# A batched trace of a matrix product: TensorE's transposes in 2-byte words with register-held addresses, and loops on three engines

## The chip, the cores and the metric

The kernel runs on one core of a Trainium2 chip. The core has five engines with instruction streams of their own, which meet through semaphores: TensorE (PE in the profile; its weight loads are shown as PEld), VectorE (DVE), ScalarE (ACT), GpSimd (POOL) and SyncE (SP). Sixteen DMA engines move data between HBM and the on-chip memory SBUF. PE writes into PSUM, which VectorE and ScalarE read. The metric is device time in microseconds; before the change it is 708.59 us, the median of 3 runs (708.46 to 708.78).

## What is computed

```python
B, N = 8, 2176
a, b: float32 [B, N, N]

prod = np.matmul(a, b)
traces = np.diagonal(prod, axis1=1, axis2=2).sum(axis=-1)   # float32 [B]
```

The trace of a product needs no product: it is the sum over i and k of a[i, k] * b[k, i]. So each element of A has to meet the element of B at the transposed place. All of A and B, 303 MB, is read once.

## The kernel before

N is 17 blocks of P = 128 rows. They come in three groups: the first 5 blocks are the "middle" (MID = 5), the other 12 are two "side" groups of 6 (SIDE = 6, MOST = 12). Within a group of m blocks, partition p holds m consecutive rows of the matrix, so that a transfer reads long runs of HBM. The transfers cast from float32 to bf16 on the way. SBUF tiles: `middle` (5 rows of 2176 per partition; it holds A's middle first and then B's middle of the same batch), `a_side` and `b_side` (12 rows each), and `at` (17 x 2176 per partition), which holds A transposed.

For each of the 8 batches:

1. POOL issues four transfers in this order: A's middle, A's side, B's middle, B's side. Each has to wait until its tile has been read: A's middle for the previous batch's product over `middle` (L160, 161), A's side for the previous batch's last transposes (L164, 165), B's middle for this batch's transposes of `middle` (L178, 179), B's side for the previous batch's second product (L183, 187). All are on one queue, in that order.
2. SP passes landings on to PE: `mid_in` when A's middle is there, `all_in` when the side is there (L139 to 145).
3. PE transposes A in a loop over the batches (L298 to 308). Its body is 26 "fills" of a PSUM tile; there are three such tiles (BUFS), released by `free0` to `free2`. For the column groups with an even number of blocks, two neighbouring bf16 numbers are taken as one 4-byte word, so that one 128 x 128 transpose moves 128 x 256 numbers; the 5 columns of the odd group go in 2-byte words. All addresses are constants. A batch has 55 transposes for the middle (8 fills) and 132 for the side (18 fills).
4. ScalarE and VectorE copy each fill into `at` (L218), ScalarE three of four, VectorE the fourth. Neither starts before both products of the previous batch are done (L217). Then each drains and adds to `at_done` (L219). Their streams are written out for all 8 batches.
5. VectorE multiplies `at` with B and sums, in one instruction per part: first with `middle` (10,880 elements per partition), then with `b_side` (26,112), L255 to 259, each sum into a column of `sums`. Each adds one to `product`.

The last batch is different, to have little left when the last byte lands. B's side comes in slices (LATE_SLICES) and the last row in three pieces (LAST_PIECES). VectorE takes some rows, and PE takes the others by accumulating matmuls of 128 x 128 blocks into `trace_ps`, whose diagonal VectorE sums (L286). The list `work` (L315 to 347) holds PE's 122 matmuls and 21 fillers (KEEP_BUSY) between them, matmuls of 512 columns into a PSUM tile that nobody reads. At the end a matmul with `ones` adds up over the partitions and SP writes the result.

## Time and profile before

| | us | where |
|---|---|---|
| median of 3 runs | 708.59 | times |
| the profiled execution | 708.71 | times |
| its span, first to last instruction | 706.6 | page |
| VectorE busy | 380.2 (54%) | page, 1 |
| PE matmul busy | 207.3 (29%) | page, 1 |
| ScalarE busy | 202.3 (29%) | page, 1 |
| HBM read | 303.04 MB, 429 GB/s | page, 3 |
| product over `b_side`, 26,112 elements | 27.36 | groups by form |
| product over `middle`, 10,880 elements | 11.49 | groups by form |
| copy of 1536 / 1280 elements, ScalarE | 1.46 / 1.23 | groups by form |
| copy of 1536 elements, VectorE | 1.76 | groups by form |

Shares are of the span. The granted clock of TensorE is 0.651 of full speed on average. A line of a timeline has the start, the time, the engine, the source line, the operation with what it writes and reads, and in brackets how long the engine sat idle before and what ended that.

### The profile page before, as it was taken

What the parts mean: (1) busy time and instruction counts of PE and PEld (TensorE: products, weight loads), DVE (VectorE), ACT (ScalarE), POOL (GpSimd) and SP (SyncE); (2) the same over time, 40 slices, a digit from 0 to 9 for tenths busy, and PEclk for the clock granted to TensorE, in tenths of its full rate; (3) what the DMA queues carried; (4) which work ended last, traced back from release to release, by engine and by line L of the source; (5) the groups of instructions that cost most, each with busy time, mean ns of one, the idle gap of its engine ahead of it and who ended that gap; (6) DMA issues with size and microseconds to landing.
All of it is one profiled execution on the core that took longest, in us unless ns stands there. A gap on an engine that the chain in (4) does not pass through costs nothing. (4 is left out here: it accounts for less than half of the span.)

```text
span 706.6 us, 3944 instructions
## 1 busy us (share of the span) xinstructions
PE 207.3 (29%) x1641; PEld 188.0 (27%) x1643; DVE 380.2 (54%) x96; ACT 202.3 (29%) x158; POOL 25.0 (4%) x47
## 2 busy tenths in 40 slices
PE   0325003450134501334013430125301353012647
PEld 0224002440123401234013430125301352012535
DVE  0105488154871539715396163961639617395268
ACT  1427002370034700246004450044500454004540
POOL 1000000000000000000000000000000000002000
PEclk9759555695557955678555785556855677555678
DMA  9999999999999999999999999999999999999997
GB/s 228 222 213 207 229 211 213 217 223 214 223 218 213 209 227 211 213 218 222 210 231 213 210 218 219 214 214 226 214 215 225 213 208 228 208 217 214 226 206 151
DMA packets 7686, 152.13 MB, mean 215 GB/s; under 512 B 642, under 2 KB 898, under 8 KB 1410
## 3 DMA queue, kind: packets, MB, share of 16 engines
q0 software_dynamic: 7536, 150.96, 99.7%
q1 hardware_dynamic: 146, 1.11, 0.5%
q8 instruction: 2, 0.03, 0.0%
q14 instruction: 2, 0.02, 0.0%
HBM read 303.04 MB, written 0.00 MB: 429 GB/s over the span
## 5 line engine op out<-in xcount | busy, mean ns | idle before, releaser
L218 ACT COPY at<-fill 128x1536 bf16<-128x1536 bf16 (+3 forms) x156 | 199.9, 1371 | 472.2 <-DVE sums L231 357.0
L231 DVE CUSTOM_DVE_ANT_0 at<-at,b_side 128x26112 bf16<-128x26112 bf16 (+4 forms) x11 | 202.9, 18460 | 84.1 <-DMA b_side<-in_b_dram 84.1
L218 DVE COPY at<-fill 128x1536 bf16<-128x1536 bf16 (+2 forms) x52 | 84.0, 1615 | 220.6 <-PE fill L307 220.2
L307 PE MATMUL fill<-identity,middle 128*128 128x128 f32 (+1 forms) x440 | 69.0, 341 | 371.3 <-PEq L305 371.2
L307 PEld LDWEIGHTS fill<-identity,middle 128*128 128x128 f32 (+1 forms) x440 | 63.5, 180 | 376.5 <-issue 376.2
L307 PE MATMUL fill<-identity,a_side 128*128 128x128 f32 (+1 forms) x1056 | 123.6, 276 | 113.4 <-PEq L305 112.8
L307 PEld LDWEIGHTS fill<-identity,a_side 128*128 128x128 f32 (+1 forms) x1056 | 113.4, 166 | 123.7 <-issue 123.3
L231 DVE CUSTOM_DVE_ANT_0 at<-at,middle 128x10880 bf16<-128x10880 bf16 x8 | 91.9, 11491 | 11.0 <-ACTq L219 11.0
L179 POOL DMA_DIRECT2D middle<-in_b_dram x8 | 4.5, 561 | 335.1 <-PE fill L307 335.1
L161 POOL DMA_DIRECT2D middle<-in_a_dram x7 | 3.9, 563 | 292.4 <-DVE sums L231 292.4
L344 PE MATMUL trace_ps<-b_side,at 128*128 128x128 bf16 x122 | 10.3, 253 | 9.4 <-DMA b_side<-in_b_dram 9.3
L344 PEld LDWEIGHTS trace_ps<-b_side,at 128*128 128x128 bf16 x122 | 9.3, 116 | 11.3 <-DMA b_side<-in_b_dram 10.9
L165 POOL DMA_DIRECT2D a_side<-in_a_dram x8 | 5.7, 711 | 0.0
L187 POOL DMA_DIRECT2D b_side<-in_b_dram x7 | 5.0, 711 | 0.0
L344 PE MATMUL fill<-at 128*128 128x512 bf16 x19 | 4.8, 379 | 0.1
L246 DVE CAST middle<-b_side 128x1088 bf16<-128x1088 f32 x1 | 0.7, 726 | 5.0 <-DMA b_side<-in_a_dram 5.0
L344 PEld LDWEIGHTS fill<-at 128*128 128x128 bf16 x21 | 1.9, 98 | 1.5
L222 ACT CAST middle<-b_side 128x1088 bf16<-128x1088 f32 x1 | 1.1, 1099 | 3.9 <-DMA b_side<-in_a_dram 3.9
L198 POOL DMA_DIRECT2D b_side<-in_b_dram x4 | 2.1, 563 | 0.0
L203 POOL DMA_DIRECT2D b_side<-in_b_dram x3 | 1.6, 593 | 0.0
L222 ACT ACT_TABLE_LOAD x1 | 1.3, 1283 | 0.9 <-SPq L135 0.9
L231 DVE DVE_READ_ACCUMULATOR2_ANT sums<- 128x1 f32 x14 | 1.2, 83 | 0.0
(17 smaller groups left out, 4.2 us busy)
## 6 DMA issues: line engine op xcount, KB each, us to landing
a_side<-in_a_dram POOLq DMA_DIRECT2D x8, 6528.0 KB, 54.6
b_side<-in_b_dram POOLq DMA_DIRECT2D x7, 6528.0 KB, 52.2
middle<-in_b_dram POOLq DMA_DIRECT2D x8, 2720.0 KB, 22.1
middle<-in_a_dram POOLq DMA_DIRECT2D x7, 2720.0 KB, 24.5
b_side<-in_b_dram POOLq DMA_DIRECT2D x1, 3264.0 KB, 37.2
middle<-in_a_dram POOLq DMA_DIRECT2D x1, 2176.0 KB, 14.8
b_side<-in_b_dram POOLq DMA_DIRECT2D x3, 544.0 KB, 46.5
b_side<-in_a_dram SPq DMA_DIRECT2D x1, 1088.0 KB, 5.1
```

The lines of the kernel that those rows point to most:

```text
L161: nc.gpsimd.dma_start(out=middle.rearrange("p (g r) k -> p g (r k)", g=1), in_=group(a[bi], 0, 1, MID),).then_inc(sem["a_mid"], 16)
L165: nc.gpsimd.dma_start(out=a_side.rearrange("p (g r) k -> p g (r k)", g=2), in_=group(a[bi], MID * P, 2, SIDE),).then_inc(sem["a_all"], 16)
L179: nc.gpsimd.dma_start(out=middle.rearrange("p (g r) k -> p g (r k)", g=1), in_=group(b[bi], 0, 1, MID),).then_inc(sem["b_mid"], 16)
L187: nc.gpsimd.dma_start(out=b_side.rearrange("p (g r) k -> p g (r k)", g=2), in_=group(b[bi], MID * P, 2, SIDE),).then_inc(sem["b_all"], 16)
L198: nc.gpsimd.dma_start(out=b_side[:, SIDE + r:SIDE + r + m, :].rearrange("p r k -> p (r k)"), in_=rows[:, r:r + m, :].rearrange("p r k -> p ...
L203: nc.gpsimd.dma_start(out=b_side[:, MOST - 1, lo:hi], in_=rows[:, SIDE - 1, lo:hi],).then_inc(sem[f"piece{len(LATE_SLICES) + k}"], 16)
L218: copy(out=dst, in_=src).then_inc(sem[f"free{i % BUFS}"], 1)
L222: nc.scalar.copy(out=middle[:, MID - 1, :half], in_=plain[:, :half]).then_inc(sem["cast"], 1)
L231: return nc.vector.tensor_tensor_reduce(out=x if out is None else out, in0=x, in1=y, scale=1.0, scalar=0.0, op0=MUL, op1=ADD, accum_out=acc,)
L246: nc.vector.tensor_copy(out=middle[:, MID - 1, half:], in_=plain[:, half:]).then_inc(sem["cast"], 1)
L307: done = nc.tensor.transpose(into, block, identity)
L344: done = nc.tensor.matmul(trace_ps if real else fill_tiles[0][:, 0:4, :], x, y, start=(n == 0 or not real), stop=(n == len(work) - 1 or no ...
```

## The change

TensorE's transposes. The tiles `middle` and `a_side` become parts of one tile `rows_a` of 18 rows: the five rows of the middle, a row of zeros, and the twelve of the side. PE loops over the batches and, inside, over 9 passes of two rows (PAIR = 2; three passes for the middle, six for the side). A pass fills three PSUM tiles, `unit0` to `unit2`, one for each column group, with 2-byte transposes alone: 34 in a pass, 306 in a batch. The address that a transpose reads is the loop's register plus a constant. Each pass takes one count of `rows_in`, of which SP gives 3 when A's middle has landed and 6 when the side has.

The copies. ScalarE copies all three units of the middle's passes and `unit0` and `unit1` of the side's; VectorE copies `unit2` of the side's. ScalarE's eight batches are one loop, and VectorE's first seven another; before, each batch's instructions were written out. POOL's waits are on `mid_read` and `side_read`, which ScalarE and VectorE give, in place of PE's count `filled`.

The products. The product over `b_side` is cut into the first 640 columns (LOW) and the rest. `low_free` follows the first part and lets ScalarE start on the middle's passes of the next batch, `act_free` follows the second and lets it start on the side's. Three sums go into `part` and are copied to `sums`. VectorE learns of B's landings through SP (`b_mid_in`, `b_all_in`).

The last batch. PE's matmuls for B's late rows become loops over the columns, a pass taking one 128 x 128 block of each row of the slice, with both operands' addresses from the loop's register; the fillers have loops of their own. The last row's 12 matmuls stay written out.

```diff
-    BUFS = 3
-    DVE_EVERY = 4
+    PAIR = 2
+    STEPS = (MID + 1 + MOST) // PAIR
+    MID_STEPS = (MID + 1) // PAIR
+    LOW = MID * P
...
-    a_side = sb.tile([P, MOST, N], bf16, tag="a_side")
+    rows_a = sb.tile([P, PAIR * STEPS, N], bf16, tag="rows_a")
+    middle, a_side = rows_a[:, 0:MID, :], rows_a[:, MID + 1:, :]
...
+    def take(engine, name, n=1):
+
+        engine.wait_ge(sem[name], n).then_inc(sem[name], -n)
...
+    def unit_copy(copy, j, step):
+
+        v, cols = columns[j]
+        row = PAIR * step
+        group_at, m, r = (0, MID, row) if step < MID_STEPS else divmod_side(row - MID - 1)
+        n = min(PAIR, m - r)
+        dst = at[:, v:v + cols, group_at:group_at + P * m].rearrange("q v (p r) -> q v p r", r=m)
+        src = units[j][:, 0:cols * PAIR, :].rearrange("q (c r) p -> q c p r", r=PAIR)
+        copy(out=dst[:, :, :, r:r + n], in_=src[:, :, :, 0:n]).then_inc(sem[f"free{j}"], 1)
...
-        for bi in range(BATCH):
-            evacuate(nc.scalar, nc.scalar.copy, bi, False)
+        with nc.Fori(0, BATCH, engines=(ACT,)):
+            take(nc.scalar, "low_free")
+            for step in range(STEPS):
+                if step == MID_STEPS:
+                    take(nc.scalar, "act_free")
+                for j in range(len(units) if step < MID_STEPS else len(units) - 1):
+                    take(nc.scalar, f"filled{j}")
+                    if step == MID_STEPS - 1 and j == len(units) - 1:
+                        nc.scalar.sem_inc(sem["mid_read"], 1)
+                        nc.scalar.sem_inc(sem["mid_copied"], 1)
+                    unit_copy(nc.scalar.copy, j, step)
+            nc.scalar.drain().then_inc(sem["at_done"], 1)
...
+        with nc.Fori(0, n_sums - PARTS + 1, PARTS, engines=(DVE,)) as column0:
+            copies_on_dve()
+            take(nc.vector, "b_mid_in")
+            rows_product(0, middle, part[:, 0:1]).then_inc(sem["product"], 1)
+            take(nc.vector, "b_all_in")
+            multiply_reduce(
+                at[:, MID:NT, 0:LOW], b_side[:, :, 0:LOW], part[:, 1:2],
+            ).then_inc(sem["product"], 1)
+            nc.vector.drain().then_inc(sem["low_free"], 1)
+            multiply_reduce(
+                at[:, MID:NT, LOW:], b_side[:, :, LOW:], part[:, 2:3],
+            ).then_inc(sem["product"], 1)
+            nc.vector.drain().then_inc(sem["act_free"], 1)
+            nc.vector.tensor_copy(
+                out=sums[:, bass.ds(column0, PARTS)], in_=part
+            ).then_inc(sem["kept"], 1)
...
+            with nc.Fori(0, PAIR * (STEPS - 1) * N + 1, PAIR * N, engines=(PE,)) as row0:
+                take(nc.tensor, "rows_in")
+                for j, (v, cols_j) in enumerate(columns):
+                    take(nc.tensor, f"free{j}")
+                    start, step = B_GROUPS[j]
+                    for c in range(cols_j):
+                        for r in range(PAIR):
+                            done = nc.tensor.transpose(
+                                units[j][:, c * PAIR + r, :],
+                                flat[:, bass.ds(row0 + (r * N + start + c), P, step=step)],
+                                identity16,
+                            )
+                    done.then_inc(sem[f"filled{j}"], 1)
...
+            def block(flat_, row):
+                at0 = c + row * N
+                return flat_[:, at0:at0 + P] if isinstance(c, int) else flat_[:, bass.ds(at0, P)]
...
+        def multiply_on_pe(landed, rows, lo, hi, busy=0):
+
+            nc.tensor.wait_ge(sem[landed[0]], landed[1])
+            with nc.Fori(lo, hi - P + 1, P, engines=(PE,)) as c:
+                for v in rows:
+                    product(v, c)
+            if busy:
+                with nc.Fori(0, busy, engines=(PE,)):
+                    x = at[:, rows[-1], :]
+                    nc.tensor.matmul(fill, x[:, 0:P], x[:, 0:4 * P], start=True, stop=True)
```

More of the change, by code (lines that the diff above doesn't have):

```diff
@@ L47 @@
     at = sb.tile([P, NT, N], bf16, tag="at")
-    a_side = sb.tile([P, MOST, N], bf16, tag="a_side")
+    rows_a = sb.tile([P, PAIR * STEPS, N], bf16, tag="rows_a")
+    middle, a_side = rows_a[:, 0:MID, :], rows_a[:, MID + 1:, :]
     b_side = sb.tile([P, MOST, N], bf16, tag="b_side")
-    middle = sb.tile([P, MID, N], bf16, tag="middle")
     identity32 = sb.tile([P, P], f32, tag="identity32")
@@ L54 @@
     ones = sb.tile([P, 1], f32, tag="ones")
-    sums = sb.tile([P, 2 * (BATCH - 1)], f32, tag="sums")
+    PARTS = 3
+    sums = sb.tile([P, PARTS * (BATCH - 1)], f32, tag="sums")
+    part = sb.tile([P, PARTS], f32, tag="part")
     late_acc = sb.tile([P, NT], f32, tag="late")
     result = sb.tile([P, BATCH], f32, tag="result")
-    fill_tiles = [ps.tile([P, 8, P], f32, tag=f"fill{j}", name=f"fill{j}") for j in range(BUFS)]
+    units = [ps.tile([P, PAIR * 8, P], bf16, tag=f"unit{j}", name=f"unit{j}") for j in range(len(B_GROUPS))]
     trace_ps = ps.tile([P, P], f32, tag="trace")
-    total = ps.tile([1, 2 * (BATCH - 1) + NT], f32, tag="total")
+    total = ps.tile([1, PARTS * (BATCH - 1) + NT], f32, tag="total")
     sem = {}
@@ L72 @@
         semaphore(f"piece{k}")
-    for name in ("cleared", "constant", "cast", "mid_in", "all_in", "filled", "at_done", "product",
-                 "traced", "summed", "reduced"):
+    for name in ("cleared", "constant", "cast", "rows_in", "mid_read", "side_read", "mid_copied",
+                 "low_free", "act_free", "at_done", "b_mid_in", "b_all_in", "product",
+                 "at_ready", "kept", "traced", "summed", "reduced"):
         semaphore(name)
-    for j in range(BUFS):
+    for j in range(len(units)):
         semaphore(f"free{j}")
+        semaphore(f"filled{j}")
+    def take(engine, name, n=1):
+        engine.wait_ge(sem[name], n).then_inc(sem[name], -n)
     def group(src, start, g, m):
@@ L82, in group @@
         return rows.rearrange("(g p r) k -> p g (r k)", g=g, r=m)
-    fills = []
-    def transposed(a_t, start, m):
-        words = a_t.bitcast(f32)
-        dst = at[:, :, start:start + P * m].rearrange("q v (p r) -> q v p r", r=m)
-        pairs, singles = [], []
-        for b_start, bm in B_GROUPS:
-            v = b_start // P
-            if bm % 2 == 0:
-                for t in range(bm // 2):
-                    pairs.append((v + 2 * t, b_start // 2 + t, bm // 2))
-            else:
-                singles += [(v + r, b_start + r, bm) for r in range(bm)]
-        for v, c0, step in pairs:
-            tile_ = fill_tiles[len(fills) % BUFS]
-            moves = [
-                (tile_[:, r, :], words[:, r, c0:c0 + step * (P - 1) + 1:step], identity32)
-                for r in range(m)
-            ]
-            fills.append((
-                moves,
-                dst[:, v:v + 2, :, :],
-                tile_[:, 0:m, :].bitcast(bf16).rearrange("q r (p s) -> q s p r", s=2),
-            ))
-        for at0 in range(0, len(singles), 16 // m):
-            some = singles[at0:at0 + 16 // m]
-            tile_ = fill_tiles[len(fills) % BUFS]
-            ps16 = tile_.bitcast(bf16).rearrange("q a b -> q (a b)")[:, 0:len(some) * m * P]
-            ps16 = ps16.rearrange("q (n r p) -> q n r p", r=m, p=P)
-            moves = [
-                (ps16[:, n, r, :], a_t[:, r, c0:c0 + step * (P - 1) + 1:step], identity16)
-                for n, (v, c0, step) in enumerate(some) for r in range(m)
-            ]
-            v0 = some[0][0]
-            fills.append((
-                moves, dst[:, v0:v0 + len(some), :, :], ps16.rearrange("q n r p -> q n p r"),
-            ))
@@ L123 @@
-    transposed(middle, 0, MID)
-    mid_fills = len(fills)
-    transposed(a_side[:, 0:SIDE, :], MID * P, SIDE)
-    transposed(a_side[:, SIDE:MOST, :], (MID + SIDE) * P, SIDE)
-    per_batch = len(fills)
-    def on_dve(bi, i):
-        return (bi * per_batch + i) % DVE_EVERY == DVE_EVERY - 1
+    columns = [(start // P, m) for start, m in B_GROUPS]
+    def unit_copy(copy, j, step):
[6 more added lines that the diff above has]
+        copy(out=dst[:, :, :, r:r + n], in_=src[:, :, :, 0:n]).then_inc(sem[f"free{j}"], 1)
@@ L132, with divmod_side @@
+    def divmod_side(row):
+        g, r = divmod(row, SIDE)
+        return (MID + g * SIDE) * P, SIDE, r
     plain = b_side.bitcast(f32).rearrange("p r k -> p (r k)")[:, :N]
     half = N // 2
+    n_sums = PARTS * (BATCH - 1)
     with tc.tile_critical(no_gpsimd_drain=True):
@@ L141 @@
             if bi == 0:
-                nc.sync.wait_ge(sem["cast"], 2)
-            nc.sync.sem_inc(sem["mid_in"], 1)
+                nc.sync.wait_ge(sem["cast"], 3)
+            nc.sync.sem_inc(sem["rows_in"], MID_STEPS)
             nc.sync.wait_ge(sem["a_all"], 16 * (bi + 1))
-            nc.sync.sem_inc(sem["all_in"], 1)
+            nc.sync.sem_inc(sem["rows_in"], STEPS - MID_STEPS)
+            if bi < BATCH - 1:
+                nc.sync.wait_ge(sem["b_mid"], 16 * (bi + 1))
+                nc.sync.sem_inc(sem["b_mid_in"], 1)
+                nc.sync.wait_ge(sem["b_all"], 16 * (bi + 1))
+                nc.sync.sem_inc(sem["b_all_in"], 1)
         nc.sync.wait_ge(sem["reduced"], 1)
@@ L159 @@
             else:
-                nc.gpsimd.wait_ge(sem["product"], 2 * bi - 1)
+                nc.gpsimd.wait_ge(sem["product"], PARTS * (bi - 1) + 1)
                 nc.gpsimd.dma_start(
@@ L163 @@
                 ).then_inc(sem["a_mid"], 16)
-                nc.gpsimd.wait_ge(sem["filled"], per_batch * bi)
+                nc.gpsimd.wait_ge(sem["side_read"], bi)
             nc.gpsimd.dma_start(
@@ L169 @@
             if bi == 0:
-                for t in (identity32, identity16):
-                    nc.gpsimd.memset(t, 0.0).then_inc(sem["cleared"], 1)
-                for k, t in enumerate((identity32, identity16)):
-                    nc.gpsimd.wait_ge(sem["cleared"], 2)
+                nc.gpsimd.memset(identity16, 0.0).then_inc(sem["cleared"], 1)
+                nc.gpsimd.memset(identity32, 0.0).then_inc(sem["cleared"], 1)
+                nc.gpsimd.wait_ge(sem["cleared"], 2)
+                for t in (identity16, identity32):
                     nc.gpsimd.affine_select(
@@ L177 @@
                     ).then_inc(sem["constant"], 1)
-            nc.gpsimd.wait_ge(sem["filled"], per_batch * bi + mid_fills)
+            nc.gpsimd.wait_ge(sem["mid_read"], bi + 1)
             nc.gpsimd.dma_start(
@@ L182 @@
             if bi:
-                nc.gpsimd.wait_ge(sem["product"], 2 * bi)
+                nc.gpsimd.wait_ge(sem["product"], PARTS * bi)
             else:
-                nc.gpsimd.wait_ge(sem["cast"], 2)
+                nc.gpsimd.wait_ge(sem["cast"], 3)
             if not last:
@@ L207 @@
         nc.gpsimd.wait_ge(sem["out"], 16)
-        def evacuate(engine, copy, bi, dve):
-            mine = [i for i in range(per_batch) if on_dve(bi, i) == dve]
-            for i in mine:
-                moves, dst, src = fills[i]
-                engine.wait_ge(sem["filled"], bi * per_batch + i + 1)
-                if bi and i == mine[0]:
-                    engine.wait_ge(sem["product"], 2 * bi)
-                copy(out=dst, in_=src).then_inc(sem[f"free{i % BUFS}"], 1)
-            engine.drain().then_inc(sem["at_done"], 1)
+        ACT = mybir.EngineType.Activation
+        DVE = mybir.EngineType.DVE
         nc.scalar.wait_ge(sem["first"], 16)
@@ L224 @@
         ).then_inc(sem["cast"], 1)
-        for bi in range(BATCH):
-            evacuate(nc.scalar, nc.scalar.copy, bi, False)
+        for name in ("low_free", "act_free"):
+            nc.scalar.sem_inc(sem[name], 1)
+        with nc.Fori(0, BATCH, engines=(ACT,)):
[10 more added lines that the diff above has]
+            nc.scalar.drain().then_inc(sem["at_done"], 1)
         def multiply_reduce(x, y, acc, out=None):
@@ L242, in rows_product, with copies_on_dve @@
             )
+        def copies_on_dve():
+            take(nc.vector, "mid_copied")
+            j = len(units) - 1
+            for step in range(MID_STEPS, STEPS):
+                take(nc.vector, f"filled{j}")
+                if step == STEPS - 1:
+                    nc.vector.sem_inc(sem["side_read"], 1)
+                unit_copy(nc.vector.tensor_copy, j, step)
+            nc.vector.drain().then_inc(sem["at_done"], 1)
+            take(nc.vector, "at_done", 2)
         nc.vector.memset(ones, 1.0)
+        nc.vector.memset(rows_a[:, MID, :], 0.0).then_inc(sem["cast"], 1)
         nc.vector.wait_ge(sem["first"], 16)
@@ L248 @@
         ).then_inc(sem["cast"], 1)
-        for bi in range(BATCH):
-            evacuate(nc.vector, nc.vector.tensor_copy, bi, True)
-            nc.vector.wait_ge(sem["at_done"], 2 * (bi + 1))
-            nc.vector.wait_ge(sem["b_mid"], 16 * (bi + 1))
-            if bi == BATCH - 1:
-                break
-            for k, (v0, rows, landed) in enumerate([(0, middle, "b_mid"), (MID, b_side, "b_all")]):
-                nc.vector.wait_ge(sem[landed], 16 * (bi + 1))
-                rows_product(v0, rows, sums[:, 2 * bi + k:2 * bi + k + 1]).then_inc(
-                    sem["product"], 1
-                )
-        nc.vector.wait_ge(sem["summed"], 1)
-        nc.vector.reduce_sum(
-            out=result[:1, 0:BATCH - 1],
-            in_=total[:, 0:2 * (BATCH - 1)].rearrange("o (b n) -> o b n", n=2),
-            axis=mybir.AxisListType.X,
-        )
+        with nc.Fori(0, n_sums - PARTS + 1, PARTS, engines=(DVE,)) as column0:
[14 more added lines that the diff above has]
+            ).then_inc(sem["kept"], 1)
+        copies_on_dve()
+        nc.vector.sem_inc(sem["at_ready"], 1)
+        nc.vector.wait_ge(sem["b_mid"], 16 * BATCH)
         cols = 0
@@ L273 @@
         rows_product(0, middle, column())
+        nc.vector.wait_ge(sem["summed"], 1)
+        nc.vector.reduce_sum(
+            out=result[:1, 0:BATCH - 1],
+            in_=total[:, 0:n_sums].rearrange("o (b n) -> o b n", n=PARTS),
+            axis=mybir.AxisListType.X,
+        )
         nc.vector.wait_ge(sem["b_all"], 16 * BATCH)
@@ L287 @@
         nc.vector.wait_ge(sem["summed"], 2)
-        early = 2 * (BATCH - 1)
         nc.vector.reduce_sum(
-            out=result[:1, BATCH - 1:BATCH], in_=total[:, early:early + cols],
+            out=result[:1, BATCH - 1:BATCH], in_=total[:, n_sums:n_sums + cols],
             axis=mybir.AxisListType.X,
@@ L295 @@
         nc.tensor.wait_ge(sem["constant"], 2)
-        for j in range(BUFS):
+        for j in range(len(units)):
             nc.tensor.sem_inc(sem[f"free{j}"], 1)
+        flat = rows_a.rearrange("p r k -> p (r k)")
         with nc.Fori(0, BATCH, engines=(PE,)):
-            for i, (moves, _, _) in enumerate(fills):
-                if i == 0:
-                    nc.tensor.wait_ge(sem["mid_in"], 1).then_inc(sem["mid_in"], -1)
-                if i == mid_fills:
-                    nc.tensor.wait_ge(sem["all_in"], 1).then_inc(sem["all_in"], -1)
-                free = sem[f"free{i % BUFS}"]
-                nc.tensor.wait_ge(free, 1).then_inc(free, -1)
-                for into, block, identity in moves:
-                    done = nc.tensor.transpose(into, block, identity)
-                done.then_inc(sem["filled"], 1)
@@ L310 @@
-        nc.tensor.wait_ge(sem["at_done"], 2 * BATCH)
-        nc.tensor.wait_ge(sem["product"], early)
-        nc.tensor.matmul(total[:, 0:early], ones, sums, start=True, stop=True).then_inc(
+            with nc.Fori(0, PAIR * (STEPS - 1) * N + 1, PAIR * N, engines=(PE,)) as row0:
[9 more added lines that the diff above has]
+                                identity16,
+                            )
+                    done.then_inc(sem[f"filled{j}"], 1)
@@ L313 @@
+        nc.tensor.wait_ge(sem["at_ready"], 1)
+        nc.tensor.wait_ge(sem["kept"], BATCH - 1)
+        nc.tensor.matmul(total[:, 0:n_sums], ones, sums, start=True, stop=True).then_inc(
             sem["summed"], 1
         )
-        work = []
-        def multiply_on_pe(landed, v, lo, hi):
-            row = b_side[:, v - MID, :]
-            for c in range(lo, hi, P):
-                work.append((landed, at[:, v, c:c + P], row[:, c:c + P], True))
-        def keep_pe_busy(v):
-            x = at[:, v, :]
-            work.extend([(None, x[:, 0:P], x[:, 0:4 * P], False)] * KEEP_BUSY.get(v, 0))
@@ L328 @@
-        for v in range(MID + DVE_ROWS, LAST):
-            multiply_on_pe(("b_all", 16 * BATCH), v, 0, N)
-            keep_pe_busy(v)
-        for k, (r, m) in enumerate(LATE_SLICES):
-            for v in range(LAST + r, LAST + r + m):
-                if v != DVE_ROW:
-                    multiply_on_pe((f"piece{k}", 16), v, 0, HALF if v == SHARED_ROW else N)
-                    keep_pe_busy(v)
-        for k, (lo, mid, hi) in enumerate(LAST_PIECES):
-            multiply_on_pe((f"piece{len(LATE_SLICES) + k}", 16), NT - 1, mid, hi)
@@ L339 @@
-        waited = None
-        for n, (landed, x, y, real) in enumerate(work):
-            if landed and landed != waited:
-                nc.tensor.wait_ge(sem[landed[0]], landed[1])
-                waited = landed
-            done = nc.tensor.matmul(
-                trace_ps if real else fill_tiles[0][:, 0:4, :], x, y,
-                start=(n == 0 or not real), stop=(n == len(work) - 1 or not real),
-            )
+        at_flat = at.rearrange("q v x -> q (v x)")
+        b_flat = b_side.rearrange("q v x -> q (v x)")
@@ new lines, with product @@
+        fill = units[0].rearrange("q b p -> q (b p)").bitcast(f32)[:, 0:4 * P]
+        def product(v, c, start=False, stop=False):
+            def block(flat_, row):
+                at0 = c + row * N
+                return flat_[:, at0:at0 + P] if isinstance(c, int) else flat_[:, bass.ds(at0, P)]
+            return nc.tensor.matmul(
+                trace_ps, block(at_flat, v), block(b_flat, v - MID), start=start, stop=stop,
+            )
+        def multiply_on_pe(landed, rows, lo, hi, busy=0):
[7 more added lines that the diff above has]
+                    nc.tensor.matmul(fill, x[:, 0:P], x[:, 0:4 * P], start=True, stop=True)
@@ new lines @@
+        first_rows = list(range(MID + DVE_ROWS, LAST))
+        nc.tensor.wait_ge(sem["b_all"], 16 * BATCH)
+        product(first_rows[0], 0, start=True)
+        for v in first_rows[1:]:
+            product(v, 0)
+        multiply_on_pe(("b_all", 16 * BATCH), first_rows, P, N, KEEP_BUSY[LAST - 1])
+        for k, (r, m) in enumerate(LATE_SLICES):
+            mine = [v for v in range(LAST + r, LAST + r + m) if v != DVE_ROW]
+            if mine:
+                v = mine[-1]
+                multiply_on_pe(
+                    (f"piece{k}", 16), mine, 0, HALF if v == SHARED_ROW else N, KEEP_BUSY.get(v, 0)
+                )
@@ L348 @@
+        for k, (lo, mid, hi) in enumerate(LAST_PIECES):
+            nc.tensor.wait_ge(sem[f"piece{len(LATE_SLICES) + k}"], 16)
+            for c in range(mid, hi, P):
+                done = product(NT - 1, c, stop=(k == len(LAST_PIECES) - 1 and c == hi - P))
         done.then_inc(sem["traced"], 1)
-        nc.tensor.wait_ge(sem["product"], early + 1)
+        nc.tensor.wait_ge(sem["product"], n_sums + 1)
         nc.tensor.matmul(
-            total[:, early:early + cols], ones, late_acc[:, 0:cols], start=True, stop=True,
+            total[:, n_sums:n_sums + cols], ones, late_acc[:, 0:cols], start=True, stop=True,
```

## The prediction

> **What bounds the kernel now.** I read the page's slices and DMA queues first, then the windows of one batch, then the timeline of that batch, and last the timeline of the final 20 us.

> ```profile
> PE   0325003450134501334013430125301353012647
> DMA  9999999999999999999999999999999999999997
> ...
> q0 software_dynamic: 7536, 150.96, 99.7%
> ```

> The transfers are at 9 in every slice but the last: the span of 706.6 us is a queue of transfers that never runs dry, with a tail of a few us. PE has at most 6 tenths in a slice. Nothing in the change takes a byte from that queue, so a gain could come only from the tail. The question is how much slower PE may become before the queue waits for it, and the timeline of the second batch answers it:

> ```profile
> 135.34 4.59 PE L307 MATMUL fill<-identity,a_side 128*128 128x128 f32 x24 [9.45 <-PEq L305]
> ...
> 140.09 1.70 PE L307 MATMUL fill<-identity,a_side 128*128 128x128 f32 x12 [0.16 <-PEq L305]
> 142.21 0.84 PE L307 MATMUL fill<-identity,a_side 128*128 128x128 bf16 x12 [0.42 <-PEq L305]
> ...
> 151.48 1.85 PE L307 MATMUL fill<-identity,a_side 128*128 128x128 bf16 x30 [0.42 <-PEq L305]
> ...
> 155.43 11.49 DVE L231 CUSTOM_DVE_ANT_0 at<-at,middle 128x10880 bf16<-128x10880 bf16 x1 [1.11 <-ACTq L219]
> ...
> 167.23 0.56 POOL L161 DMA_DIRECT2D middle<-in_a_dram  x1 [39.77 <-DVE sums L231]
> ...
> 178.69 27.36 DVE L231 CUSTOM_DVE_ANT_0 at<-at,b_side 128x26112 bf16<-128x26112 bf16 x1 [11.76 <-DMA b_side<-in_b_dram]
> ```

> The first column is the start. The side rows of A land at 135.3; their stage (transposes, copies, drain) ends at 155.4, so it takes 20.1 us. The middle product follows, and only then, at 167.2, is the next batch's middle of A issued. The transfer ahead of it in the queue lands at 178.7, so 11.5 us are to spare. Over the seven batches this gap is 12.5, 11.5, 11.4, 11.7, 11.7, 11.3 and 11.8, mean 11.7. Part of it is the lead that a transfer needs. The first SP load of 1088 KB (SBUF) lands 5.1 us after issue, and 1.11 MB at the page's 429 GB/s are 2.6, so the lead is at most 2.5 us. The side stage may thus grow by 9.2 us, to 29.3, before the queue runs dry; each us beyond costs 7 us, once per batch.

> The second bound is the tail, where the last rows of B meet A on PE:

> ```profile
> 687.06 5.30 PE L344 MATMUL trace_ps<-b_side,at 128*128 128x128 bf16 x51 [7.49 <-DMA b_side<-in_b_dram]
> ...
> 692.42 1.46 PE L344 MATMUL fill<-at 128*128 128x512 bf16 x6
> ...
> 693.71 2.06 PE L344 MATMUL trace_ps<-b_side,at 128*128 128x128 bf16 x34
> ...
> 700.46 0.62 PE L344 MATMUL trace_ps<-b_side,at 128*128 128x128 bf16 x8 [1.14 <-DMA b_side<-in_b_dram]
> ...
> 702.17 1.33 PE L344 MATMUL trace_ps<-b_side,at 128*128 128x128 bf16 x12 [0.66 <-DMA b_side<-in_b_dram]
> ```

> From 687.06 to 703.5 PE is all but full; it waits 1.1 and 0.7 us in the end. What is added to this row of matmuls by more than about 1.8 us comes out at the end of the kernel.

> **The change, part by part.** Unit prices first, since the trace before has no register-addressed matmul and its one loop edge per batch lies inside a wait.
> A static 2-byte transpose: 1.85 us / 30 = 0.062 us, the pair of load and matmul, so 0.031 per instruction that PE's sequencer hands over. [...]
> An address from a register needs register operations ahead of it. Lower bound: one instruction at 0.031. Upper: 0.16, the shortest gap of PE that a wait on its sequencer leaves (140.09). I take two instructions, a sum and a scaling, 0.062, by the row it is nearest to, since a register operation waits for no other engine. So r = 0.062 (0.031 to 0.16).
> A loop edge (counter, compare, jump, refill): lower two instructions, 0.062; upper 0.42, the usual gap after a release (151.48). Neither is like it, so the middle: e = 0.24.

> *Transposes, side stage.* Removed: 132 per batch, 72 of 4-byte words (0.14 each: 1.70/12) and 60 of 2 bytes. Added: 6 passes of 34, that is 204, each 0.062 + r = 0.124: 25.3 us. Per pass a loop edge and four takes of a semaphore at 0.06 (two instructions), 0.24 + 0.24, six times: 2.9. Behind the last one the release gap, the last copy and the drain, 0.3 + 1.7 + 1.1 = 3.1. Sum 31.3 us against 20.1. With the lower prices 23.9, with the upper ones 52.3. Against 29.3 allowed the stage is 2.0 us late, and what is late next is the issue of A's middle, behind which A's side is queued on POOL: 7 x 2.0 = 14 us (lower 0, upper 161).

> *Copies.* Side stage: ScalarE 6 x (1.23 + 1.46) = 16.2 us, VectorE 6 x 1.76 = 10.6, both hidden under PE's 28; without that cover ScalarE's would set the stage at about 20. Middle stage: ScalarE takes all nine, 2 x (1.23 + 1.46 + 1.46) and three half ones at 0.86, 10.9 us. They may start earlier than before: the product over B's side is cut, and its first part, 7680 of 26112 elements, frees what they write after 27.36 x 7680/26112 = 8.1 us, where ScalarE's wait of 51.8 us now ends after 27.4. With PE's 68 transposes behind the first three units (68 x 0.124 + 2 x 0.48 = 9.4) the middle of B is issued about 15 us earlier than at 126.2. A's side lands 9.1 us after that issue, so the queue was never short there: worth 0.

> *VectorE's loop.* Two more read-outs of 0.08, a copy of three numbers, two drains and a loop edge: at most 5 us, a drain put at the 1.9 us of the longest wait before L231. VectorE has 12.98 us idle ahead of 138.19 and takes them there: 0. *SP and POOL.* B's landing now passes through SP, and POOL's releases come from ScalarE and VectorE instead of PE: one hop, up to 0.42 us, on waits that have 9 to 13 us to spare: 0. On the middle product the hop comes long after B's middle has landed. The start of the kernel stays: rows of A land at 16.6 and 47.4 as now.

> *The tail.* Both operands of a looped matmul are register-addressed: 0.062 + 2r = 0.186. Loops: 16 passes over three rows, 48 x 0.186 + 16e = 12.8; 17 over two, 10.4; 17 over one, 7.2; 8 over one, 3.4. The 21 fillers in loops of their own: 0.243 each by the row at 692.42 or 0.062 + e = 0.302, the larger, 6.3. Sum 40.2, the twelve static ones 0.7 behind. PE may start when b_side has landed (687.06) and A is ready: 659.05 + 31.3 = 690.4. End 690.4 + 40.2 + 0.7 = 731.2, against 703.5: **27.7 us** (6.2 at the lower prices, 84 at the upper). VectorE's own chain, 23.2 us behind A being ready, ends at 714 and is covered by PE.

> Sum against the profiled run's own time, 708.71 (span 706.6 and 2.1 around it; 0.12 over the median of the runs): 708.7 + 14 + 27.7 = **750 us**.

> [...] The windows put the granted clock at 0.91 while the transposes run:

> ```profile
> 135.00:156.00 21.00, 15.38 (x132) 13.98 (x132) 8.55 (x6) 17.11 (x13) 0.00 (x0) 0.91 1.01 217
> ```

> [...]

> **The rivals.**
> *Cheap registers (0.20).* One instruction per address and 0.062 per edge: no stall, and the tail 6.2 us late: 715, up to 725 for prices halfway to mine. For it: the sequencer is idle most of the time and may run ahead. Against: in the tail PE is full, so there is nothing to run ahead of.
> *The side stage becomes the bound (0.09).* Near the upper prices, 52.3 us per stage: 708.7 + 161 + 84 = 954; I count all above 820 to it. For it: 204 addresses per batch in a stage with 9 us to spare. Against: 0.16 contains a semaphore's way, which a register operation has not.
> *Not slower (0.11), 708.6.* The mechanism: PE's sequencer works out addresses and edges while the array still runs and while PE waits for the pieces, so that each loop of the tail ends at its piece's landing. It decides if the 79 edges and 220 addresses of the tail add less than 1.8 us in sight. For it: 51 matmuls in 5.30 us are 0.104 each, well above 0.062, so the first 48 have cover. Against: the next 34 run at 0.061 and have none. Even then the gain is small: behind the last transfer (702.8) lie 3.8 us, so nothing under 704.9 is possible.
> The change might also not loop at all on PE; then it would time as this rival.

> **How the numbers follow.** Forecast (725 to 820): 0.60; its own time 750. The rivals have 0.20, 0.09 and 0.11. The range 714 to 820 leaves out the not slower case and the bound beyond, 0.2 in all. A measurement of this kernel can tell 0.2% (1.4 us) from no change. Slower 0.89, within 0.2% 0.06, faster 0.05, the last two from the not slower case.

> **What would show it.** In the profile after: the gap between successive transposes (0.124, or 0.09, or 0.22); the side stage from the landing of a_side to the middle product (31 us); idle DMA at the issue of A's middle once per batch, 2 us or none, as digits below 9; and the last matmul of trace_ps 28 us behind the last landing less what the stalls moved. The prediction is wrong if transposes come faster than 0.09 us, if the tail's loops end within a few us of the last landing, or if code is loaded again at loop edges (the instruction queues hold 4 packets now).

## The result and the profile after

The changed kernel takes 791.9 us (median of 4 runs, 791.3 to 792.7) against 708.6: a ratio of 1.1175, with a 95% interval of 1.1156 to 1.1195. The forecast was slower, at 750 us. The direction was right, and the forecast loss was half of the measured one: 41 us against 83. The profiled execution took 791.3 us, with a span of 789.0.

The first view is the changed kernel's page, the busy tenths in 40 slices and the main queue:

```profile
DMA  9999699997999979997999979999799979999600
...
q0 software_dynamic: 7536, 150.96, 89.9%
```

The transfers were at 9 in all slices but the last before. Now there is one slice of 6 or 7 in each batch, seven in all, and a 6 and two zeros at the end. The same packets now fill 89.9% of the span. So the loss has two parts: the queue runs dry once per batch, and there is work left when it has ended.

Next is the timeline of the second batch of the changed kernel (start, time, engine, line, operation; idle before and its releaser in brackets), with the stretches left out in which the passes repeat:

```profile
140.54 4.78 PE L316 MATMUL unit<-identity,rows_a 128*128 128x128 bf16 x34 [14.71 <-PEq L87]
...
145.89 4.81 PE L316 MATMUL unit<-identity,rows_a 128*128 128x128 bf16 x34 [0.56 <-PEq L87]
...
167.34 4.81 PE L316 MATMUL unit<-identity,rows_a 128*128 128x128 bf16 x34 [0.61 <-PEq L87]
...
174.55 11.49 DVE L220 CUSTOM_DVE_ANT_0 at<-at,rows_a 128x10880 bf16<-128x10880 bf16 x1 [0.40 <-DVEq L87]
...
186.35 0.56 POOL L146 DMA_DIRECT2D rows_a<-in_a_dram  x1 [58.82 <-DVE part L220]
```

The side rows land at 140.54. A pass of 34 transposes comes every 5.36 us: PE is at work for 4.78 and idle for 0.57 between passes. The 4.78 divided by 34 is 0.141 us, the figure that the expectations below use for one transpose; it has the stops between the units of a pass in it, which the weight loads further down tell apart. The middle product starts at 174.55, so the side stage takes 34.0 us (20.1 before), and A's next middle is issued 45.8 us behind the landing. The windows of the same stretch show the queue running dry; the last three columns are the granted clock, the DMA share and GB/s:

```profile
140.50:174.50 34.00, 28.67 (x204) 24.94 (x204) 10.55 (x6) 16.66 (x12) 0.00 (x0) 0.60 1.02 219
174.50:186.00 11.50, 0.00 (x0) 0.00 (x0) 11.45 (x3) 0.00 (x0) 0.00 (x0) 0.50 0.68 145
186.00:192.00 6.00, 0.00 (x0) 0.00 (x0) 6.00 (x3) 0.00 (x0) 1.27 (x2) 0.50 0.88 163
```

During the middle product the share falls to 0.68, as no transfer is left to run; behind the issue at 186.35 it returns. The first middle product starts at 81.8 and the eighth at 732.8: a batch takes 93.0 us where it took 87.3 (from one product over `b_side` to the next in the kernel before). Seven stalls of 5.7 us are 40 us.

The tail of the changed kernel, from the same kind of view:

```profile
732.85 0.82 PE L338 MATMUL trace_ps<-b_side,at 128*128 128x128 bf16 x6
...
746.15 0.63 PE L338 MATMUL trace_ps<-b_side,at 128*128 x3 [0.33 <-issue]
747.11 0.59 PE L338 MATMUL trace_ps<-b_side,at 128*128 x3 [0.33 <-issue]
...
762.32 0.44 PE L338 MATMUL trace_ps<-b_side,at 128*128 x2 [0.33 <-issue]
763.12 0.44 PE L338 MATMUL trace_ps<-b_side,at 128*128 x2 [0.37 <-issue]
...
775.39 0.26 PE L338 MATMUL trace_ps<-b_side,at 128*128 x1 [0.34 <-issue]
776.00 0.26 PE L338 MATMUL trace_ps<-b_side,at 128*128 x1 [0.34 <-issue]
...
785.85 0.29 DVE L220 CUSTOM_DVE_ANT_0 diagonal<-identity,trace_ps 128x128 bf16<-128x128 f32 x1 [30.23 <-PE trace_ps L338]
```

A loop pass takes about 0.92 us with three matmuls, 0.77 with two and 0.61 with one, with PE idle in each, released by "issue": PE waits for nothing else that the profile shows than its own instructions. The row takes 53.0 us (732.85 to 785.8) where it took 16.4. VectorE waits 30.2 us for it.

The loss adds up. A's last side lands 39.8 us later (698.85 for 659.08), the tail starts another 6.0 us later (34.0 us behind that landing, where 28.0 us were between it and b_side's landing at 687.06), and it takes 36.6 us longer: 82.4, the difference of the spans.

### The profile page after: what moved, and what is told of

Read it like the earlier page. It is cut to its first block, busy times and chain, and to the rows that moved or that the text cites. A ratio compares the mean times of both kernels' runs of the same rounds, so it can differ in the third digit from the quotient of the medians.

```text
span 789.0 us, 9286 instructions
## 1 busy us (share of the span) xinstructions
PE 377.0 (48%) x2593; PEld 314.2 (40%) x2595; DVE 383.2 (49%) x114; ACT 283.9 (36%) x170; POOL 25.1 (3%) x47
## 3 DMA queue, kind: packets, MB, share of 16 engines
q0 software_dynamic: 7536, 150.96, 89.9%
q1 hardware_dynamic: 146, 1.11, 0.4%
## 5 line engine op out<-in xcount | busy, mean ns | idle before, releaser
L316 PE MATMUL unit<-identity,rows_a 128*128 128x128 bf16 x2448 | 343.4, 294 | 387.0 <-PEq L87 386.1
L316 PEld LDWEIGHTS unit<-identity,rows_a 128*128 x2448 | 299.2, 123 | 431.1 <-issue 414.2
L104 ACT COPY at<-unit 128x1280 bf16<-128x1280 bf16 (+2 forms) x168 | 281.5, 1757 | 441.5 <-ACTq L87 441.5
L104 DVE COPY at<-unit 128x1536 bf16<-128x1536 bf16 x48 | 84.4, 1758 | 361.6 <-DVEq L87 361.6
L220 DVE CUSTOM_DVE_ANT_1 at<-at,b_side 128x7680 bf16<-128x7680 bf16 (+1 forms) x14 | 192.6, 13756 | 1.2 <-issue 1.2
L220 DVE CUSTOM_DVE_ANT_0 at<-at,rows_a 128x10880 bf16<-128x10880 bf16 x8 | 91.9, 11493 | 3.2 <-DVEq L87 3.2
L338 PE MATMUL trace_ps<-b_side,at 128*128 (+1 forms) x122 | 25.2, 278 | 19.6 <-issue 19.6
L338 PEld LDWEIGHTS trace_ps<-b_side,at 128*128 (+1 forms) x122 | 12.6, 108 | 32.1 <-issue 28.7
L146 POOL DMA_DIRECT2D rows_a<-in_a_dram x7 | 3.9, 564 | 412.0 <-DVE part L220 412.0
L220 DVE CUSTOM_DVE_ANT_0 diagonal<-identity,trace_ps 128x128 bf16<-128x128 f32 x1 | 0.3, 289 | 30.2 <-PE trace_ps L338 30.2
L220 DVE CUSTOM_DVE_ANT_0 at<-at,b_side 128x6528 bf16<-128x6528 bf16 (+3 forms) x4 | 11.3, 2874 | 0.0
L150 POOL DMA_DIRECT2D rows_a<-in_a_dram x8 | 5.7, 711 | 0.0
```

The lines of the kernel that those rows point to most:

```text
L104: copy(out=dst[:, :, :, r:r + n], in_=src[:, :, :, 0:n]).then_inc(sem[f"free{j}"], 1)
L146: nc.gpsimd.dma_start(out=middle.rearrange("p (g r) k -> p g (r k)", g=1), in_=group(a[bi], 0, 1, MID),).then_inc(sem["a_mid"], 16)
L150: nc.gpsimd.dma_start(out=a_side.rearrange("p (g r) k -> p g (r k)", g=2), in_=group(a[bi], MID * P, 2, SIDE),).then_inc(sem["a_all"], 16)
L220: return nc.vector.tensor_tensor_reduce(out=x if out is None else out, in0=x, in1=y, scale=1.0, scalar=0.0, op0=MUL, op1=ADD, accum_out=acc,)
L316: done = nc.tensor.transpose(units[j][:, c * PAIR + r, :], flat[:, bass.ds(row0 + (r * N + start + c), P, step=step)], identity16,)
L338: return nc.tensor.matmul(trace_ps, block(at_flat, v), block(b_flat, v - MID), start=start, stop=stop,)
```

## The experiments

All are edits of the changed kernel. A time stands beside the kernel before on the same chip, 708.7 us in each group.

**The tail written out**: the last batch's matmuls with constant addresses.

```diff
-            with nc.Fori(lo, hi - P + 1, P, engines=(PE,)) as c:
+            for c in range(lo, hi, P):
                 for v in rows:
                     product(v, c)
...
-                with nc.Fori(0, busy, engines=(PE,)):
...
+            for _ in range(busy):
...
```

> The last batch's matmuls on TensorE are written out again with constant addresses; the transposes stay in their loop. Theory (register operations and loop edges on TensorE's sequencer): the tail's row of matmuls shrinks from 52.8 us to some 13 to 16, VectorE's own chain behind A being ready sets the end instead, and since its last instruction now waits 30.2 us for trace_ps, the time falls by 30.2 to about 762 us. Rival (the tail is late only because A is late, and its loops cost little): 785 us or more.

Measured: 759.7 us (ratio 1.072, 1.070 to 1.074). The row of matmuls takes 13.1 us, and VectorE's chain behind the late A sets the end. The row is 40 us shorter than the changed kernel's 53.0, and the time falls by 32: the 30.2 that VectorE had waited, and 1.3 by which A's last side landed earlier in this execution (697.52 for 698.85). The rest of the 40 is hidden, as VectorE's chain is the next bound.

**The passes written out**: the nine passes of transposes with constant addresses.

```diff
-            with nc.Fori(0, PAIR * (STEPS - 1) * N + 1, PAIR * N, engines=(PE,)) as row0:
+            for row0 in range(0, PAIR * STEPS * N, PAIR * N):
...
-                                flat[:, bass.ds(row0 + (r * N + start + c), P, step=step)],
+                                flat[:, row0 + r * N + start + c:
+                                     row0 + r * N + start + c + step * (P - 1) + 1:step],
```

> The nine passes of 2-byte transposes are written out with constant addresses; the tail keeps its loops. Theory (register operations): the gap between transposes falls from 0.141 us to about 0.062, the side stage from 34.0 us to some 20, set by ScalarE's copies; all seven stalls (40 us) go and TensorE's tail starts at the landing of b_side, 687 us: 746 us. [...] Rival 2 (the cut product, the loops on ScalarE and VectorE or the passes through SP make the stalls): they stay, 785 us or more.

Measured: 749.1 us (1.057, 1.055 to 1.059). The side stage takes 20.8 us and no slice of the DMA row but the last few is under 9: the stalls are gone, so they do not come from the cut product, the loops on ScalarE and VectorE or the passes through SP. The 3 us over the expectation lie in one loop of the tail: the 17 passes over one row take 0.82 us each instead of 0.61, while the other loops keep their pace. In most of these passes PE is idle for 0.55 to 0.60 us ahead of its matmul, where it is 0.34 in the changed kernel. Why was not tried.

**Both written out.**

> Both parts on TensorE are written out with constant addresses; the loops on ScalarE and VectorE, the cut product and the 2-byte words stay. Theory: the register-held addresses and the loop edges on TensorE are the whole cost, so 708.6 us within 1.5. Rival (the other parts cost something of their own that the two large losses cover): 712 us or more.

Measured: 708.6 us over 10 runs, ratio 0.9998 (0.9989 to 1.0008). What is left of the change, the 2-byte words, the loops on ScalarE and VectorE, the cut product and the hops through SP, costs nothing that can be measured.

**One address**: all transposes of a unit read the same register-held address.

```diff
-                    start, step = B_GROUPS[j]
+                    start, step = 0, B_GROUPS[j][1]
...
-                                flat[:, bass.ds(row0 + (r * N + start + c), P, step=step)],
+                                flat[:, bass.ds(row0, P, step=step)],
```

> All transposes of a unit read one and the same register-held address, so that a pass needs two register instructions instead of 34 (the transposed blocks are thus not those of A). Loop, 2-byte words and register-addressed loads stay. Theory (the register instruction is the price): gap 0.062 us, side stage about 20 us, time 746 us as with written-out passes. Rival 1 (the register-addressed load itself is slow): gap 0.14 us, 792 us. [...]

Measured: 746.0 us (one run). This is the test that separates the register instruction from the register-addressed load. The answer for the line of the transposes counts the instructions of PE's queues (PEldq is its sequencer) with the least, median and greatest time in ns; first the changed kernel, then this one:

```profile
L316 PEldq FUSED_REGOPS  x2448: 42/46/62, 16.9 to 730.0; - x189
L316 PEld LDWEIGHTS unit<-identity,rows_a x2448: 117/124/128, 17.0 to 730.1; 128*128 x189
```

```profile
L316 PEld LDWEIGHTS unit<-identity,rows_a x2448: 116/126/153, 16.7 to 676.6; 128*128 x189
...
L316 PEldq FUSED_REGOPS  x72: 37/37/48, 16.6 to 674.0; - x72
L316 PEldq ALU_OP  x72: 36/36/42, 16.9 to 674.9; - x72
```

In the changed kernel each of the 2448 transposes has a register instruction of its own, recorded at 46 ns. Here there are two for a pass. The loads are register-addressed as before. What the instruction costs is read from the weight loads of a pass, whose three units have 10, 12 and 12; first the changed kernel, then this one:

```profile
151.26 1.26 PEld L316 LDWEIGHTS unit<-identity,rows_a 128*128 x10 [0.75 <-issue]
...
152.68 1.53 PEld L316 LDWEIGHTS unit<-identity,rows_a 128*128 x12 [0.16 <-issue]
...
154.36 1.50 PEld L316 LDWEIGHTS unit<-identity,rows_a 128*128 x12 [0.15 <-issue]
```

```profile
151.25 0.73 PEld L316 LDWEIGHTS unit<-identity,rows_a 128*128 x12 [0.36 <-issue]
```

One load lasts about 0.125 us in both, so from the first start to the last there are 1.375 and 0.605 us for 11 steps: 0.125 and 0.055 us from load to load. The price belongs to the register instruction, 0.070 us in the stream for a record of 0.046, and not to the register-addressed load.

The changed kernel's rows show a second cost. Between two units PE takes a semaphore (`free`), and the loads stop for 0.15 to 0.16 us there, although the copies have long emptied the unit (in the first pass of the second batch's side, ScalarE's copy of `unit0` ends at 143.39, and the next load for it starts at 145.88). The take alone does not do it. In the kernel with the passes written out, where the addresses are constant, 22 loads with such a take among them run in 1.28 us, and the first two rows above need 2.95 for 22:

```profile
150.08 1.28 PEld L316 LDWEIGHTS unit<-identity,rows_a 128*128 128x128 bf16 x22 [0.69 <-issue]
```

In the changed kernel the take has a register instruction behind it, that of the next transpose. Between two passes, with two takes and the loop edge, the loads stop for 0.75 us.

**Three passes per edge**: the inner loop runs three times over three passes.

```diff
-            with nc.Fori(0, PAIR * (STEPS - 1) * N + 1, PAIR * N, engines=(PE,)) as row0:
-                take(nc.tensor, "rows_in")
+            with nc.Fori(0, 2 * 3 * PAIR * N + 1, 3 * PAIR * N, engines=(PE,)) as row0:
+                for sub in range(3):
+                    take(nc.tensor, "rows_in")
...
```

> TensorE's inner loop makes three passes per edge: three edges in a batch instead of nine, with as many register instructions. The pass boundary of the changed kernel costs 0.58 us, of which the four takes of a semaphore may be 0.24 by the prediction's price. Theory (the edge is the rest): the side stage falls by 4 x 0.34 = 1.4 us to 32.6, and the time by eight times that (seven stalls, one late start of the tail), 11 us, to 781. Rival (the boundary is the takes, or the release of the units): 790 to 792 us.

Measured: 778.7 us (1.099, 1.097 to 1.101). The timeline of PE in this kernel's second batch has both kinds of boundary:

```profile
149.37 4.79 PE L318 MATMUL unit<-identity,rows_a 128*128 128x128 bf16 x34 [0.20 <-PEq L87]
154.72 4.74 PE L318 MATMUL unit<-identity,rows_a 128*128 128x128 bf16 x34 [0.57 <-PEq L87]
159.66 9.66 PE L318 MATMUL unit<-identity,rows_a 128*128 128x128 bf16 x68 [0.20 <-PEq L87]
```

With an edge the next pass starts 5.35 us behind the last (149.37 to 154.72), without one 4.94 (154.72 to 159.66). The side stage has four edges fewer and is 1.8 us shorter, so an edge costs 0.41 to 0.45 us, more than PE's idle gaps of 0.57 and 0.20 suggest; that is why the kernel came out 2 us below the expectation. The stage is 32.2 us and a batch 91.2, so 1.8 us less stage is 1.8 us less stall. The line through both kernels, 34.0 with 5.7 and 32.2 with 3.9, meets zero at a stage of 28.3 us.

**The side in halves**: A's side rows in two transfers, each releasing three passes. Loops and register addresses stay.

```diff
...
-            nc.sync.wait_ge(sem["a_all"], 16 * (bi + 1))
-            nc.sync.sem_inc(sem["rows_in"], STEPS - MID_STEPS)
+            for name in ("a_half", "a_all"):
+                nc.sync.wait_ge(sem[name], 16 * (bi + 1))
+                nc.sync.sem_inc(sem["rows_in"], SIDE // PAIR)
...
-            nc.gpsimd.dma_start(
-                out=a_side.rearrange("p (g r) k -> p g (r k)", g=2),
-                in_=group(a[bi], MID * P, 2, SIDE),
-            ).then_inc(sem["a_all"], 16)
+            for g, name in enumerate(("a_half", "a_all")):
+                nc.gpsimd.dma_start(
+                    out=a_side[:, g * SIDE:(g + 1) * SIDE, :].rearrange("p (g r) k -> p g (r k)", g=1),
+                    in_=group(a[bi], (MID + g * SIDE) * P, 1, SIDE),
+                ).then_inc(sem[name], 16)
```

> The side rows of A come in two transfers of six rows, and the passes over the first half may start when it has landed, some 15.6 us before the rest. All loops and register addresses stay. Theory (a stall comes only from how late the side stage ends behind the whole landing): three passes of 5.36 us and the copies are left behind the second landing, 18 us instead of 34; no stall, the tail starts at 687 us, the time is 792 - 40 - 6 = 746 us. Rival (slow passes hold up the queue elsewhere, as through the middle's passes or ScalarE's copies): above 755 us.

Measured: 745.4 us (1.052, 1.050 to 1.054), with 87.3 us for a batch. The transposes are as slow as in the changed kernel; only their start has moved, and the stalls are gone. So the slow transposes cost nothing in themselves here; what cost was how late the stage ended.

**No fillers**: the 21 matmuls that nobody reads are left out of the tail.

```diff
-            if busy:
+            if False:
```

> The 21 fillers of the tail are left out. Theory (the tail is bound by the sequencer's register operations and edges, at 0.385 us for a pass of a filler loop): 8.1 us less, 784 us. Rival (the fillers hold up TensorE's clock and the matmuls behind them need it): less than 4 us gained.

Measured: 783.2 us (1.105, 1.103 to 1.107), 8.6 less than the changed kernel. The passes with three and two matmuls stay at about 0.92 and 0.77 us, with the clock at 0.50 of full speed instead of 0.53. So neither the fillers nor the clock sets the pace of these loops; what is left is the sequencer's own instructions.

**Halves, and the tail written out.**

> The side rows in halves and the tail written out; the transposes stay in their loop with a register instruction each. Theory: 0.141 us per transpose is hidden in full under the transfers once the stage may start earlier, so 708.6 us within 1.5. Rival (the loop costs something besides the stalls): 712 us or more.

Measured: 708.7 us over 10 runs, ratio 0.9999 (0.9990 to 1.0009). In the page's slices of this kernel PE is busy, and in good time:

```profile
PE   0886018850188502885028840388303883048847
```

PE is busy for 51% of the span instead of 29, and the time is that of the kernel before. No version tried is faster than that one: the transfers bound it.

## Why the prediction was right in kind and half in size

**What bounds the kernel**: right. The queue of transfers gives the time, the stalls come at the issue of A's middle once per batch, and the tail adds the rest. The kernels with both parts written out (708.6 us) and with the halves and the tail written out (708.7) show it.

**What was costed at nothing**: right in sum. The cut product, ScalarE's and VectorE's loops and the hops on SP cost nothing together: 708.6 us with both parts written out. One term was off under its cover: the copies of the middle stage take 18.5 us instead of 10.9, and B's middle is issued at 126.2, at the old time and not 15 us earlier. It has 14 us to spare before A's side lands, so nothing came of it.

**The price of an address**: right in size. A transpose was put at 0.062 + r = 0.124 us, and the loads of a unit come every 0.125. Part of this is luck, as r was put together as "two instructions, a sum and a scaling", where the trace has one fused instruction.

**The pass boundary**: the step that failed first, and the largest error. It was put at "a loop edge and four takes of a semaphore at 0.06", 0.48 us a pass and 2.9 in the stage. By the rows of loads the 34 transposes of a pass take 4.29 us and the stops 1.06: two of 0.155 and one of 0.75. So a take ahead of a register instruction costs some 0.15 us and not 0.06, and the edge, 0.75 less two takes, 0.45 and not 0.24. The stage then adds up to 25.7 for its transposes (25.3 forecast), 5.6 for five stops between passes and twelve inside them (2.9 forecast), and 2.7 behind the last load (3.1 forecast): 34.0 us, not 31.3. Seven times 2.7 is 19 of the 26 us by which the stalls were forecast too small. The nearest row for a take stood in the prediction's own timeline: the gap of 0.16 at 140.09 is behind one, and it was used as the upper bound of an address.

**The lead of a transfer**: the other 7 us of the stalls. The queue forgives a stage of 28.3 us, by the line through two kernels, where 29.3 were allowed. The lead was taken as at most 2.5 us from the first load of an empty queue; against the mean slack of 11.7 it is 3.5 at this place.

The two errors are small, and the stall is what is left over a threshold: 34.0 - 28.3 in place of 31.3 - 29.3. A stage 9% longer and a threshold 3% lower made it 5.7 us in place of 2.0, close to three times.

**A loop edge in the tail**: the same mis-sized edge. It was put at "the middle: e = 0.24", between 0.062 and 0.42. The passes of 0.92, 0.77 and 0.61 us fit 0.46 us for a pass and 0.153 for each matmul in it, so the edge was above its upper end. A matmul with two addresses was dearer in the forecast (0.186); in the trace both addresses share one fused instruction, 107 records (49 and 58, by their lines) for the 107 looped matmuls. (The prediction also counts 220 addresses here; the 107 looped matmuls have 214.) The tail's row takes 53.0 us and not 40.9: 58 edges add 12.8, the fillers, at 0.39 a pass and not 0.30, 1.8, and the twelve static matmuls 0.8, while the cheaper matmuls give 3.5 back.

Of the 41 us that the forecast lacked, the pass boundary thus has about 22 (19 in the stalls, 2.7 in the tail's later start), the row of the tail 12 and the lead 7.

The size of an edge could have been bounded better before. The prediction said that the trace has no register-addressed matmul and that its one loop edge lies inside a wait. The wait hides the edge from the groups and the timeline, but the answer for the loop's own line in the trace of the kernel before counts the sequencer's instructions:

```profile
L298 PEldq ALU_OP  x8: 36/36/42, 65.3 to 676.8; - x8
L298 PEldq COMPARE_BRANCH  x8: 83/215/230, 65.4 to 676.9; - x8
```

A register operation at 0.036 us and a branch with a median of 0.215 stand there. If the two follow each other, as the sequencer's records in the changed kernel do (the first ones start at 21.5 and 21.6 us), an edge is at least 0.251 us; the loops of the tail also have a first address to work out behind each edge, 0.078 in the changed kernel's record. By these records the lower bound of 0.062 for an edge was far too low, and the middle of 0.24 was below the new lower bound.

**The rivals.** Cheap registers and not slower fell with the first pass in the trace, where the loads come every 0.125 us and not under 0.09, and with the tail's row of 53.0 us. The side stage as the sole bound did not come either: stalls and tail share the loss, 40 and 43 us.

**The granted clock and the branch.** The granted clock is 0.50 with PE idle (174.5 to 186 in the changed kernel). With transposes alone it is 0.92 in the stage of the kernel with both parts written out, 0.85 with one address (both 0.055 us from load to load), and 0.60 in the changed kernel (0.125). So in these windows it was higher with transposes than without them, and highest where they are dense; what parts 0.92 from 0.85 was not tried. The compare-and-branch records of PE have a median of 208 to 215 ns, and a whole edge cost 0.41 to 0.46 us in the stream.

## What to carry to other kernels

## What was not expected of the hardware

ScalarE's copies of the middle's last pass, which write single 2-byte elements 10 bytes apart, take longer than the mean copy of twice the size, which writes pairs. From the groups of the changed kernel by form:

```profile
L104 ACT COPY at<-unit 128x1536 bf16<-128x1536 bf16 x80 | 144.1, 1836 | 19.6 <-ACTq L87 19.6
...
L104 ACT COPY at<-unit 128x768 bf16<-128x768 bf16 x16 | 36.6, 2446 | 0.0
L104 ACT COPY at<-unit 128x640 bf16<-128x640 bf16 x8 | 15.8, 1970 | 0.0
```

The mean of one, the number behind the comma, is 2446 ns for 768 elements and 1836 for 1536. VectorE's long product, which runs beside part of these copies, is not the cause: in the first batch VectorE does nothing from 7.1 to 52.7 us, and there the copies of 768 still take 2.45 us, those of 640 1.98. The mean of 1836 mixes two kinds. In the middle stage (window 18 to 37.2), where pairs start 10 bytes apart, 1536 elements take 2.33 us and 1280 take 1.97; in the side stage (140 to 173), where they start 12 bytes apart, 1.50 and 1.28. So in the middle a lone element costs about what a pair does, and all of its copies are slow. No run changed the spacing alone, so that it is the cause is not shown.
